# Large matmul operands placed at multiples of 256 bytes, and one preparation step moved, in a two-layer decoder trunk

## The chip, the cores and the metric

The kernel runs on one core of one Trainium2 chip. The metric is the device time of one execution in microseconds (us), the median of several runs. The profiled execution is one more run of the same program, with the hardware profiler on.

A core has a matrix engine (TensorE: PE for its products, PEld for its loads of the stationary operand), a vector engine (VectorE, DVE), an activation engine (ScalarE, ACT), GpSimd (POOL) and SyncE (SP), which here issues nearly all DMA transfers. A product of the matrix engine has a stationary operand of up to 128x128, loaded first, and a moving operand of 128 partitions and up to 512 columns, which streams through. Both are read from the on-chip memory (SBUF), which has 128 partitions; a tile has one address, the same in every partition. "At 64" below means an address that is 64 bytes past a multiple of 256.

## The reference

Two layers over 256 tokens of width 1024. Each layer runs four token mixers on the same input, gates and sums them, projects, and normalizes. Layer 0 then has a dense SwiGLU, layer 1 a mixture of eight experts, of which each token takes two. Both add a gated per-layer embedding.

```
for i in range(DEPTH):                       # 2
    h = x @ w_in[i]                          # 1024 x 6752
    ... s5, mla, hgrn2, retention            # four mixers, 256 wide each
    mixed = sum(gates * branches) @ w_o[i]
    x = layer_norm(ALPHA * x + mixed, ...)
    if i % 2 == 0:
        f = swiglu(x, ff_w_gate, ff_w_up, ff_w_down)       # 1024 -> 3584 -> 1024
    else:
        f = moe_swiglu(x, moe_router, moe_w_gate, moe_w_up, moe_w_down)  # 8 experts, top 2
    ple = sigmoid(x @ ple_w_gate[i]) * (p[i] @ ple_w_proj[i])
    x = layer_norm(ALPHA * x + f + ple, ...)
```

All inputs are float32.

## The kernel before

**Products.** Every large product is split in three. An operand is written as a high part `hi` in the type float32r and a rest `lo = x - hi`, also float32r; `mm3` (L246) issues hi·hi (L248), then one product with a `lo` (L249), then the other (L250), all into the same bank of PSUM. A float32r product reads 4 bytes per column and partition. In the four mixers' inputs, in the gates and in the dense SwiGLU's first part the weights are stationary and 256 columns of activations move; in the value and gate projections, the output projection, the dense second part and all of the experts 512 columns of weights move and the activations are stationary. Small products (attention scores, transposes, scans) are plain float32.

**Weights.** `Stream` (L132) carries the weights. A piece of 1 MB comes by DMA from SP into a slot `raw` (L157). `ahead` (L178) splits it: ACT writes `hi` (L191), DVE writes `lo` (L193). A slot of `raw` is reloaded as soon as its piece is split. In the experts' stage a piece is 128x2048, there are nine slots of `raw`, and four pairs `whi`, `wlo`; `whi` lies mostly in the pool `wp`, `wlo` in the pool `more`.

**Experts.** `experts` (L484) goes through 8 experts in four steps `j` of 8, 8, 8 and 4 pieces of gate and up products (`up`, bank `pff`), each followed by the down products of the step before (`down`, bank `pdn`, 4, 4, 4 and 2 pieces). That is 42 pieces of 12 products each per expert, 336 pieces and 4032 products in all, 2688 of them `pff` and 1344 `pdn`. The order of PE, DVE and ACT is here the order of the program (`manual_schedule`, L1797). After each piece `pump` (L226) lets the side generators go one step; a generator that yields n is left alone for n pieces. One side generator is `turn` (L1515), started after each `up`: it multiplies gate and up (L1517, DVE), transposes the result with PE (bank `ftp`, L1522) and splits it into `hth`, `htl`.

**The step that is moved.** `prepare` (L1651) readies the next expert's tokens. It is started before step 1 of an expert and must be done before the next expert's step 0 (`before`, L1807). In this order it builds a one-hot matrix on DVE (`oh`, L1656) with small copies on POOL (L1657), multiplies it with PE (`ohp`, L1662), copies the indices out (DVE, L1669; ACT, L1671), issues a gather of 128 rows from POOL (L1695), yields 6, and then twice transposes four blocks with PE (bank `gat`, L1687) and splits them on ACT and DVE (L565, L566) into `ghl`, the stationary operand of the next expert.

**Placement.** Pools are laid out one after the other, and a tile takes the next multiple of 32 bytes. On the left `cst` starts at 16512 and has 548 float32 columns; `mhalf` (L283), 32 bytes, follows at 18720; so the pool `wp` begins at 18752, which is at 64. `wp` and `act` hold multiples of 8192 bytes, so `raw`, `whi`, `xh`, `xl`, `ghl` and the rows are all at 64. The pool `sm` of small tiles has 2080 bytes, so that the pools of a stage behind it (the mixers' outputs `y`, `hth`, `htl`, the dense stage's additional `wparts`) are at 96. On the right, pools grow down from 229344, which is at 224: the S5 matrices, and in layer 1 the pool `more` with 11 slots of 8192 bytes (`wlo`, further `raw`) and two of 4096 (`ye`, among them the first expert's `gh`, `gl`) are at 224. The temporary tiles of the mixers are at 0, and only plain float32 products read them.

Of the kernel before, what the change touches and what calls it, by code (L numbers as in the profile page):

```python
# [10 lines left out]
F32 = mybir.dt.float32  # L11
F32R = mybir.dt.float32r
I32 = mybir.dt.int32
# [7 lines left out]
P = 128  # L21
T = 256
NT = 2
# [6 lines left out]
EPS = 1e-5  # L30
ALPHA = (2 * DEPTH) ** 0.25
MAGIC = 12582912.0


C_E = 0
# [62 lines left out]
def tile_trunk(ctx, tc, x, p, positions, w_in, s5_a_re, s5_a_im, s5_log_dt, s5_b_re, s5_b_im, s5_c_re, s5_c_im,  # L98
# [5 lines left out]
    V, G_, S, PE = nc.vector, nc.gpsimd, nc.scalar, nc.tensor  # L104
# [4 lines left out]
    const = ctx.enter_context(tc.tile_pool(name="const", bufs=1))  # L109
    wp = ctx.enter_context(tc.tile_pool(name="wp", bufs=1))  # L110
    act = ctx.enter_context(tc.tile_pool(name="act", bufs=1))
    sm = ctx.enter_context(tc.tile_pool(name="sm", bufs=4))
    drp = ctx.enter_context(tc.tile_pool(name="drp", bufs=1, space=bass.MemoryType.DRAM))
    ph = {}
    ps = ctx.enter_context(tc.tile_pool(name="ps", bufs=1, space=PSUM))

    def dump(name, ap):
        if dbg and name in dbg:
            nc.sync.dma_start(dbg[name], ap)

    def mm_bank(name):
        return ps.tile([P, 512], F32, tag="mm", bufs=4, name=name)

    def ax_bank(name):
        return ps.tile([P, 512], F32, tag="ax", bufs=4, name=name)
# [145 lines left out]
    mixc = mix_pool.__enter__()  # L271
# [8 lines left out]
    mcol = lambda c, n: cmix[:, c - C_MIX:c - C_MIX + n]  # L280
    m64 = mcol(C_M64, 2)
    m16 = mcol(C_M16, 2)
    mhalf = const.tile([P, 8], F32, name="mhalf")  # L283
    cols = mixc.tile([P, P], F32, name="cols")
    d_col = lambda i: cols[:, 64 + 8 * i:72 + 8 * i]
    qg_col = lambda i: (cols[:, 100 + i:101 + i], cols[0:64, 102 + i:103 + i])
# [12 lines left out]
    def reduce_angle(r, ang, k):  # L299

        V.tensor_scalar(k, ang, 1.0 / (2 * math.pi), MAGIC, op0=OP.mult, op1=OP.add)
        V.tensor_scalar(k, k, -MAGIC, None, op0=OP.add)
        V.scalar_tensor_tensor(r, k, -TWO_PI[0], ang, op0=OP.mult, op1=OP.add)
# [12 lines left out]

    stg = mixc.tile([P, P], F32, name="stg")
    sst = mixc.tile([P, 32], F32, name="sst")
    posi = mixc.tile([P, NT], I32, name="posi")

    def small_loads(q):

# [142 lines left out]
    def s5_setup(i, s5, pad, bank, turn):  # L465
# [82 lines left out]
            eng.tensor_tensor(o, o, w, op=op)  # L548
            yield 1
        yield 1  # L550
        toep = mixc.tile([P, 8, 4, 32], F32, tag="s5to", bufs=1, name="toep")
        yield from turn()
        for b2 in range(2):
            tb = bank("tb")
# [8 lines left out]
    def split_out(hi, lo, src, scale=None):  # L563
        if scale is None:
            S.activation(hi, src, AF.Copy)  # L565
            V.tensor_sub(lo, src, hi.bitcast(F32))  # L566
        else:
            S.activation(hi, src, AF.Copy, scale=scale)
            V.scalar_tensor_tensor(lo, src, scale, hi.bitcast(F32), op0=OP.mult, op1=OP.subtract)
# [621 lines left out]
    def mixers(i, xh, xl, s5, ready, end):  # L1191

        res, hl, rl = {}, {}, {}
        def prepare_s5():

            pad = act.tile([P, 2048], F32, tag="x", bufs=1, name="pad")
            yield from setup(ready, pad)
            yield from s5_setup(0, s5, pad, ax_bank, lambda: ())
# [68 lines left out]
        def branch(n, first=False, last=False):  # L1267
            drain_side(gens[n], "mixer %d of layer %d" % (n, i))
            y = res[n]
            dump("y%s%d" % ("abcd"[n], i), y[0].bitcast(F32))  # L1270
            if last:
                parts.extend(new_parts())
            for h in range(2):
                wh, wl = ws.take("br", n, i)
                for b in range(2):
                    o = mm_bank("pbr")
                    for f in range(2):
                        fs = slice((2 * b + f) * P, (2 * b + f + 1) * P)
                        for kk in range(2):
                            mm3(o[:, f * T:(f + 1) * T], wh[:, kk, fs], wl[:, kk, fs], y[0][:, kk, :], y[1][:, kk, :],  # L1280
                                kk == 0 and f == 0, kk == 1 and f == 1)
                    tv, av = flat(thg[n], 2 * h + b), flat(thg[ORDER[0]], 2 * h + b)
                    V.scalar_tensor_tensor(tv, tv, 1.0, o, op0=OP.add, op1=OP.mult)
                    if not first:
                        (V if last else G_).tensor_tensor(av, av, tv, op=OP.add)
                    if last:
                        split_out(flat(parts[0], 2 * h + b), flat(parts[1], 2 * h + b), av, 0.5)
                pump()
                finished()
            ph["branches"] += 1  # L1290
# [267 lines left out]
    def dense(i, xh, xl, pj, pr, gb, s5):  # L1558

        for c in range(4):  # L1560
            ple_quarter(i, c, xh, xl, pj, pr)
        res = []

        def add(tt, h, b):
            hs = slice(512 * h, 512 * h + 512)
            V.tensor_add(pr[:, tt, hs], pr[:, tt, hs], b)

        def end(u, todo):
            res.extend(ln_parts(pr, add, gb, todo, u["acc"], [fill0, lambda: drain_side(s5_)]))

        def turn():

            while not ph["spare"]:
                yield 1


        pad = ph["pool"].tile([P, 2, D], F32, tag="gain1", bufs=1, name="pad").rearrange("p a d -> p (a d)")
        s5_ = start_side(s5_setup(i + 1, s5, pad, mm_bank, turn))

        def fill0():  # L1580
            ph["spare"] = True
            for _ in range(4):
                step_side(s5_)


        ffn([dict(x=(xh, xl), take=lambda w, *k, **kw: ws.take(w, 0, *k, **kw))], NT, lambda n, j: None, end)
        return res
# [9 lines left out]
    def moe(i, xt, xh, xl, pj, pr, wr, more, gains, write):  # L1597
# [53 lines left out]
        def prepare(pcol, scol, wcol, e):  # L1651

            oh = ph["pool"].tile([P, NT, P], F32, tag="oh", bufs=1, name="oh")
            wt = sm.tile([P, NT, 2], F32, tag="wt", bufs=2, name="wt")
            for tt in range(NT):
                V.tensor_scalar(oh[:, tt, :], iota, pcol(tt), scol(tt), op0=OP.is_equal, op1=OP.mult)  # L1656
                G_.tensor_copy(wt[:, tt, 0:1], wcol(tt))  # L1657
                G_.tensor_copy(wt[:, tt, 1:2], cst[:, C_TOK + tt:C_TOK + tt + 1])
            yield 1
            tp = ax_bank("ohp")  # L1660
            for tt in range(NT):
                PE.matmul(tp[:, 256:258], oh[:, tt, :], wt[:, tt, :], start=tt == 0, stop=tt == 1)  # L1662
            if e.get("turned"):
                e["ohT"] = ohT = ph["pool"].tile([P, T], F32R, tag="ohT", bufs=1, name="ohT")
                for tt in range(NT):
                    PE.transpose(tp[:, tt * P:tt * P + P], oh[:, tt, :], ident)
            yield 1
            idx = sm.tile([P, 1], U32, tag="idx", bufs=2, name="idx")
            V.tensor_copy(idx, tp[:, 257:258])  # L1669
            e["ws"] = sm.tile([P, 1], F32, tag="ws", bufs=2, name="ws")  # L1670
            S.copy(e["ws"], tp[:, 256:257])  # L1671
            xg = rows_of(x_rows, idx, e.get("place", 0), "xg")
            if e.get("turned"):
                S.copy(ohT, tp[:, 0:256])
            yield 3 if e.get("first") else 6
            if e.get("first"):
                gh, gl = (ph["more"][0].tile([P, KD, P], F32R, tag="ye", bufs=2, name="g" + t) for t in "hl")
            else:

                both = act.tile([P, 2, KD, P], F32R, tag="xl" if e.get("odd") else "xh", bufs=1, name="ghl")  # L1680
                gh, gl = both[:, 0], both[:, 1]
            e["x"] = gh, gl
            for k4 in range(2):
                b = ax_bank("gat")
                for k in range(4):
                    ks = slice((4 * k4 + k) * P, (4 * k4 + k + 1) * P)
                    PE.transpose(b[:, k * P:(k + 1) * P], xg[:, ks], ident)  # L1687
                yield 1
                split_out(*(t[:, 4 * k4:4 * k4 + 4, :].rearrange("p k t -> p (k t)") for t in (gh, gl)), b)
                yield 1  # L1690

        def rows_of(src, idx, place, name):

            t = places[place]
            G_.indirect_dma_start(t, None, src[:, :], bass.IndirectOffsetOnAxis(ap=idx, axis=0))  # L1695
            return t
# [94 lines left out]

        for tt in range(NT):
            nc.gpsimd.dma_start(x_rows[tt * P:(tt + 1) * P, :], xt[:, tt, :])
        both_ = act.tile([P, NT, D], F32, tag="x", bufs=1, name="rows")
        places = [both_[:, n, :] for n in range(2)]
        state = {"p": start_side(first_rows())}
# [28 lines left out]
        with tc.If(many > P):  # L1825
# [4 lines left out]
            with tc.For_i(0, NE, 1) as ei:  # L1830
# [5 lines left out]
                more = Stream()  # L1836
# [51 lines left out]
    for i in range(DEPTH):  # L1888
# [33 lines left out]
        more = ph["more"] if last else (ph["pool"], "more", 2)  # L1922
# [3 lines left out]
        wr = router(i) if i % 2 else None  # L1926
        xt, xh, xl, pr = out_proj(i, mh, ml, xt, pj)
        dump("x1_%d" % i, xt)
        if i % 2 == 0:
            gb = gain_rows(ln2_g, ln2_b, i, (ph["pool"], "gain2", 1))  # L1930
# [3 lines left out]
        else:  # L1934
            moe(i, xt, xh, xl, pj, pr, wr, more, lambda: gain_rows(ln2_g, ln2_b, i, ws.free.pop(0)), write)
        dump("x2_%d" % i, pr)
        pool.__exit__(None, None, None)

# [31 lines left out]
```

## Time and profile before

| | us |
|---|---|
| median of 3 runs | 1856.11 |
| the runs | 1855.95 to 1862.53 |
| the profiled execution | 1855.93 |
| its span, first to last instruction | 1854.1 |

Columns and marks of the profile: "busy" is the time in which an engine has an instruction running. A product's duration includes its way through the array, and the next one starts long before it ends, so durations of products overlap and do not tell the pace; the distance of their starts does. In a timeline a row has the start, the length, the engine, the line and the operation, what is written from what, the shape, and how many were merged. "PE ... <- DVE ..." in a list of waits reads: PE waited for DVE.

### The profile page before, as it was taken

What the parts mean: (1) busy time and instruction counts of PE and PEld (TensorE: products, weight loads), DVE (VectorE), ACT (ScalarE), POOL (GpSimd) and SP (SyncE); (2) the same over time, 40 slices, a digit from 0 to 9 for tenths busy, and PEclk for the clock granted to TensorE, in tenths of its full rate; (3) what the DMA queues carried; (4) which work ended last, traced back from release to release, by engine and by line L of the source; (5) the groups of instructions that cost most, each with busy time, mean ns of one, the idle gap of its engine ahead of it and who ended that gap; (6) DMA issues with size and microseconds to landing.
All of it is one profiled execution on the core that took longest, in us unless ns stands there. A gap on an engine that the chain in (4) does not pass through costs nothing.

```text
span 1854.1 us, 25642 instructions
## 1 busy us (share of the span) xinstructions
PE 1798.2 (97%) x10285; PEld 1550.8 (84%) x10285; DVE 1443.1 (78%) x1344; ACT 1125.3 (61%) x1095; POOL 275.6 (15%) x286
## 2 busy tenths in 40 slices
PE   8999999999998999989999999999999999999996
PEld 7889989999987989978788788787887878878885
DVE  7966787645466965778888888888888888888896
ACT  5544455444445464546777777777776777777773
POOL 2746338100022210322000000000000000000001
PEclk9999999999999999999999999999999999999998
DMA  7443475555543346847999999999999999999991
GB/s 244 137 140 115 143 255 188 186 190 191 184 148 134 107 148 247 315 148 260 375 357 374 357 370 382 353 371 364 368 381 357 368 380 357 369 361 368 385 395 50
DMA packets 164115, 506.09 MB, mean 273 GB/s; under 512 B 15340, under 2 KB 30228, under 8 KB 149652
## 3 DMA queue, kind: packets, MB, share of 16 engines
q1 hardware_dynamic: 160900, 493.36, 72.7%
q0 software_dynamic: 2080, 7.35, 1.0%
q10 hardware_dynamic: 1008, 3.67, 0.5%
q8 instruction: 82, 1.34, 0.3%
q14 instruction: 45, 0.37, 0.1%
HBM read 497.52 MB, written 6.82 MB: 272 GB/s over the span
## 4 chain that ended last, share of the span: by engine, by line
PE 77%; DVE 5%; ACT 2%; issue 1%; POOL 0%; POOLq 0%; DVEq 0%; ACTq 0%
PE pff L248 14%; PE pff L250 14%; PE pff L249 14%; PE pdn L250 7%; PE pdn L248 7%; PE pdn L249 6%; PE pgt L250 2%; PE pgt L248 2%; PE pgt L249 1%; PE ftp L1522 1%; DVE wlo L193 1%; ACT whi L191 1%; DVE wparts L193 1%; DVE xt L603 1%; PE ppg L248 1%
## 5 line engine op out<-in xcount | busy, mean ns | idle before, releaser
L193 DVE TENSOR_TENSOR wlo<-raw,whi 128x2048 fp32r<-128x2048 f32 x336 | 768.5, 2292 | 129.3 <-ACT whi L191 120.4
L191 ACT ACTIVATE whi<-raw 128x2048 fp32r<-128x2048 f32 x336 | 643.4, 1918 | 244.5 <-PE pff L250 140.3
L193 DVE TENSOR_TENSOR wparts<-raw,wparts 128x1024 fp32r<-128x1024 f32 (+1 forms) x235 | 306.1, 1309 | 185.3 <-ACT wparts L191 184.3
L191 ACT ACTIVATE wparts<-raw 128x1024 fp32r<-128x1024 f32 (+1 forms) x244 | 254.4, 1049 | 252.3 <-PE pff L250 79.3
L248 PE MATMUL pff<-whi,ghl 128*128 128x512 f32 x784 | 312.8, 399 | 0.0
L250 PE MATMUL pff<-whi,ghl 128*128 128x512 f32 x784 | 309.1, 394 | 0.0
L249 PE MATMUL pff<-wlo,ghl 128*128 128x512 f32 x784 | 308.7, 394 | 0.0
L248 PE MATMUL pdn<-whi,hth 128*128 128x512 f32 x448 | 178.8, 399 | 0.0
L250 PEld LDWEIGHTS pff<-whi,ghl 128*128 128x128 f32 x784 | 147.2, 188 | 36.0
L250 PE MATMUL pdn<-whi,htl 128*128 128x512 f32 x448 | 177.0, 395 | 0.0
L249 PE MATMUL pdn<-wlo,hth 128*128 128x512 f32 x448 | 175.5, 392 | 0.0
L249 PEld LDWEIGHTS pff<-wlo,ghl 128*128 128x128 f32 x784 | 147.3, 188 | 33.7
L248 PEld LDWEIGHTS pff<-whi,ghl 128*128 128x128 f32 x784 | 147.2, 188 | 33.5
L250 PE MATMUL pgt<-xh,wparts 128*128 128x256 f32 x512 | 146.4, 287 | 1.7 <-DVE wparts L193 1.7
L249 PE MATMUL pgt<-xl,wparts 128*128 128x256 f32 x512 | 146.3, 286 | 0.0
L248 PE MATMUL pgt<-xh,wparts 128*128 128x256 f32 x512 | 146.2, 286 | 0.0
L249 PE MATMUL pff<-xl,wparts 128*128 128x256 f32 x448 | 126.4, 282 | 0.0
L248 PE MATMUL pff<-xh,wparts 128*128 128x256 f32 x448 | 126.3, 282 | 0.0
L250 PE MATMUL pff<-xh,wparts 128*128 128x256 f32 x448 | 126.3, 282 | 0.0
L250 PEld LDWEIGHTS pgt<-xh,wparts 128*128 128x128 f32 x512 | 98.5, 193 | 2.6 <-DVE wparts L193 1.9
L250 PEld LDWEIGHTS pdn<-whi,htl 128*128 128x128 f32 x448 | 84.2, 188 | 19.5
L249 PEld LDWEIGHTS pdn<-wlo,hth 128*128 128x128 f32 x448 | 84.3, 188 | 18.9
(570 smaller groups left out, 3135.4 us busy)
## 6 DMA issues: line engine op xcount, KB each, us to landing
raw<-in_moe_w_gate_dram SPq DMA_DIRECT2D x112, 1024.0 KB, 7.3
raw<-in_moe_w_up_dram SPq DMA_DIRECT2D x112, 1024.0 KB, 7.6
raw<-in_moe_w_down_dram SPq DMA_DIRECT2D x112, 1024.0 KB, 7.3
raw<-in_w_in_dram SPq DMA_DIRECT2D x49, 1024.0 KB, 5.0
raw<-in_ff_w_gate_dram SPq DMA_DIRECT2D x14, 1024.0 KB, 5.1
raw<-in_ff_w_up_dram SPq DMA_DIRECT2D x14, 1024.0 KB, 5.1
raw<-in_ff_w_down_dram SPq DMA_DIRECT2D x14, 1024.0 KB, 4.8
raw<-in_w_branch_dram SPq DMA_DIRECT2D x8, 1024.0 KB, 4.9
```

The source lines that it names most:

```text
L191: S.activation(hi, src, AF.Copy)
L193: eng.tensor_tensor(lo, src, hi.bitcast(F32), op=OP.subtract)
L248: PE.matmul(o, ah, bh, start=start, stop=False)
L249: PE.matmul(o, ah, bl, start=False, stop=False)
L250: PE.matmul(o, al, bh, start=False, stop=stop)
L603: V.scalar_tensor_tensor(dst[:, tt, hs], src[:, tt, hs], mv[:, 0:1], gb[0][h], op0=OP.subtract, op1=OP.mult)
L1522: PE.transpose(tp[:, c * P:(c + 1) * P], g[h][:, c, :], ident)
```

## The change

Two things are done. Five places get padding: `mhalf` grows from 8 to 56 columns (32 to 224 bytes), `sm` gets a tile of 224 bytes, `posi` grows by 8 columns, `toep` by 56, and the pool `more` gets a tile of 224 bytes, which comes behind its others. The new tiles are cleared with one DVE instruction each, so that they are used. And in `prepare`, for every expert but the first, a `yield 2` is put ahead of the one-hot matrix, and the `yield 6` after the gather becomes `yield 10`.

```diff
+PAD = 56
@@ tile_trunk
+    V.memset(sm.tile([P, PAD], F32, tag="pad", bufs=1, name="smpad"), 0.0)
@@
-    mhalf = const.tile([P, 8], F32, name="mhalf")
+    mhalf = const.tile([P, PAD], F32, name="mhalf")
@@
-    posi = mixc.tile([P, NT], I32, name="posi")
+    posi = mixc.tile([P, NT + 8], I32, name="posi")[:, 0:NT]
@@ s5_setup
-        toep = mixc.tile([P, 8, 4, 32], F32, tag="s5to", bufs=1, name="toep")
+        toep = mixc.tile([P, 1024 + PAD], F32, tag="s5to", bufs=1, name="toep")[:, 0:1024]
+        toep = toep.rearrange("p (g b c) -> p g b c", g=8, b=4)
@@ prepare
             wt = sm.tile([P, NT, 2], F32, tag="wt", bufs=2, name="wt")
+            if not e.get("first"):
+                yield 2
             for tt in range(NT):
@@
-            yield 3 if e.get("first") else 6
+            yield 3 if e.get("first") else 10
@@ moe
             nc.gpsimd.dma_start(x_rows[tt * P:(tt + 1) * P, :], xt[:, tt, :])
+        V.memset(ph["more"][0].tile([P, PAD], F32, tag="pad", bufs=1, name="morepad"), 0.0)
```

## Rows read from the trace of the kernel before

**Rows 1.** The page: busy time, share, instructions; the chain that ended last.
```profile
PE 1798.2 (97%) x10285; PEld 1550.8 (84%) x10285; DVE 1443.1 (78%) x1344; ACT 1125.3 (61%) x1095; POOL 275.6 (15%) x286
PE 77%; DVE 5%; ACT 2%; issue 1%; POOL 0%; POOLq 0%; DVEq 0%; ACTq 0%
```
**Rows 2.** Windows: length, busy PE PEld DVE ACT POOL, PE clock, DMA share, GB/s.
```profile
0.00:853.00 853.00, 822.34 (x5933) 761.57 (x5934) 586.73 (x817) 413.42 (x607) 250.34 (x247) 0.99 0.52 178
853.00:1835.00 982.00, 972.38 (x4348) 788.02 (x4346) 846.95 (x512) 710.40 (x486) 20.17 (x32) 1.00 0.95 360
```
**Rows 3.** Waits from 853 to 1835 us: total us, times, longest.
```profile
ACT whi L191 <- PE pff L250: 140.3, 163, 2.2
DVE wlo L193 <- ACT whi L191: 119.3, 208, 2.3
...
PE ftp L1522 <- DVE ghl L566: 8.9, 7, 1.4
```
**Rows 4.** Timeline of PE: one run of 96 `pff`, one of 47 `pdn`.
```profile
1709.15 0.39 PE L248 MATMUL pff<-whi,ghl 128*128 128x512 f32 x1
...
1731.27 0.39 PE L250 MATMUL pff<-whi,ghl 128*128 128x512 f32 x1
...
1823.98 0.40 PE L249 MATMUL pdn<-wlo,hth 128*128 128x512 f32 x1
...
1834.64 0.40 PE L250 MATMUL pdn<-whi,htl 128*128 128x512 f32 x1
```
**Rows 5.** Timeline of PE: 36 products of 512 columns, all operands at 64.
```profile
650.46 0.39 PE L248 MATMUL pqk<-wparts,xh 128*128 128x512 f32 x1
...
658.40 0.39 PE L250 MATMUL pqk<-wparts,xl 128*128 128x512 f32 x1
```
**Rows 6.** Timeline of PE: 192 products, then 96 with the moving operand at 96.
```profile
750.44 0.28 PE L248 MATMUL pgt<-xh,wparts 128*128 128x256 f32 x1
...
773.36 0.28 PE L250 MATMUL pgt<-xh,wparts 128*128 128x256 f32 x1
773.48 0.28 PE L248 MATMUL pbr<-ydh,wparts 128*128 128x256 f32 x1
...
784.67 0.28 PE L250 MATMUL pbr<-yah,wparts 128*128 128x256 f32 x1
```
**Rows 7.** Timeline of PE: 384 products of the dense stage's first part.
```profile
306.40 0.28 PE L248 MATMUL pff<-xh,wparts 128*128 128x256 f32 x1
...
352.06 0.28 PE L250 MATMUL pff<-xh,wparts 128*128 128x256 f32 x1
```
**Rows 8.** Plain float32 of 512 columns at 96: timeline, then the tile's duration.
```profile
1834.87 3.60 PE L1782 MATMUL cmb<-yef,ohT 128*128 128x512 f32 x8
...
L1782 PE MATMUL cmb<-yef,ohT x8: 590/592/595, 1834.9 to 1837.9; 128*128 128x512 f32 x8
```
**Rows 9.** Timeline of PE: products of 32 columns, paced by their weight loads.
```profile
169.84 0.39 PE L536 MATMUL kp<-pad,s5vr 128*128 128x32 f32 x2
...
170.51 0.39 PE L537 MATMUL kp<-pad,s5vi 128*128 128x32 f32 x2
```
**Rows 10.** Timeline of PE: the router, 8 stationary columns, 256 moving ones at 64.
```profile
826.67 0.28 PE L248 MATMUL lp<-xh,wrh 128*8 128x256 f32 x1
...
827.25 0.28 PE L250 MATMUL lp<-xh,wrl 128*8 128x256 f32 x1
```
**Rows 11.** Timelines of PE and of DVE where the prepared rows are split.
```profile
1032.04 0.60 PE L1522 MATMUL ftp<-cst,ffg 128*128 128x128 f32 x4
...
1027.79 2.29 DVE L193 TENSOR_TENSOR wlo<-raw,whi 128x2048 fp32r<-128x2048 f32 x1
1029.99 0.68 DVE L566 TENSOR_TENSOR ghl<-gat,ghl 128x512 fp32r<-128x512 f32 x1
1030.59 0.68 DVE L1517 TENSOR_TENSOR ffg<-ffg,pff 128x512 f32<-128x512 f32 x1
```
**Rows 12.** The tile `rows`, which the gathers write: us from issue to landing.
```profile
DMA to landing us min/median/max: 4.3/7.6/11.1
```

## The prediction

> **What bounds the kernel now.** I read the page first, to see which engine is never free: PE is busy 97% of the span and makes 77% of the chain that ended last [rows 1]. Then the windows, because a share of the whole span is a mean over stages: before the experts (0 to 853 us) PE is busy 822 of 853 us and DVE 587; with the experts (853 to 1835 us) PE is busy 972 of 982 us, DVE 847, and the DMAs 95% at 360 GB/s, at a granted clock of 1.00, which is 2.4 GHz [rows 2]. Three things are near their limit there, so the waits decide: ACT waits for PE to give a pair of weight parts back, DVE waits for ACT, and PE waits for nobody but 8.9 us in seven places; no wait of ACT for a weight's DMA is in the list [rows 3]. So PE sets the end, in both halves, and what counts is the pace of its products: the distance of their starts.
>
> That pace is read from the first and the last of a run. With the experts 96 `pff` take 22.12 us in 95 distances, 232.8 ns each, and 47 `pdn` 10.66 us in 46, 231.7 ns [rows 4]. 512 columns at 2.4 GHz are 213.3 ns, so each product carries some 19 ns beside its columns. Where all operands are at 64 the same shape takes 7.94/35 = 226.9 ns [rows 5]. With 256 columns (106.7 ns) it is 22.92/191 = 120.0 ns with everything at 64 and 11.19/95 = 117.8 ns with the moving operand at 96 [rows 6], and 45.66/383 = 119.2 ns in the dense stage, whose stationary parts are partly at 96 [rows 7]. So the surplus at 64 is 13.3 ns whether 256 or 512 columns move, it hangs on the placement, and no placement in the trace is without it: no moving float32r operand stands at a multiple of 256.
>
> **How large it is without a surplus.** Three rows bound it. Plain float32 products pass 512 columns at half the rate: eight take 3.60 us, the last 0.592, so (3.60-0.592)/7 = 430 ns against 426.7, 3 ns over, although both operands are at 96 [rows 8]. Changing the stationary operand therefore costs 3 ns, not 13; the rest of the surplus comes with reading 4 bytes per column at the full rate. Products of 32 columns show the pace of the weight loads alone: 0.67 us for six, 112 ns [rows 9]. And the router, which loads 8 columns instead of 128, still takes 0.58/5 = 116 ns for 256 columns moving from 64 [rows 10], 9 more than the columns: the moving operand's reading has a surplus with hardly a load beside it. 13.3 ns are 32 columns, 128 bytes: what one block more of 128 bytes would take, and a row of 1024 or 2048 bytes that begins at 64 touches one more such block than one at 0. That fits 120.0 = 288/2.4 and 226.7 = 544/2.4. I take this reading: at 0 the surplus goes, and 216 ns (213.3+3) remain for 512 columns, 112 for 256 (there the load's pace is the floor).
>
> **The change part by part.** *Padding.* `wp` moves from 18752 to 18944, which is 74 x 256; `sm` grows to 2304 bytes, so the stage pools follow from 96 to 0; on the right 224 bytes bring `more` from 224 to 0, and 256 bytes in all keep the mixers' temporary tiles at 0. So every float32r operand of a large product comes to 0.
> - Experts: 2688 x (232.8-216) + 1344 x (231.7-216) = 45.2 + 21.1 = 66 us. What is late next is DVE: its 847 us of work would stand in some 910, 93%, where a piece's 2.29 us [rows 11] must fit into 12 x 216 = 2.6 us beside the smaller instructions. I take 57 us of the 66. The DMAs would have to bring 390 GB/s instead of 360; no wait names them now [rows 2, 3], so I charge nothing, and up to 15 us if they fall behind.
> - Before the experts: 256 columns, 1824 gate and input products at 120.0, 1344 dense ones at 119.2, 768 branch and embedding products at about 117.8 [rows 6, 7]: 14.6 + 9.7 + 4.5 = 29 us. 512 columns: 288 at 226.9 and 576 between this and 232.8, say 230 [rows 4, 5]: 3.1 + 8.1 = 11 us. 96 products of 352 columns: 1 us. Together 41 us on PE. DVE and ACT chains of the mixers lie beside it, and PE is 31 us short of fully busy there [rows 2], so some of the gain turns into waits; I take three quarters, 31 us.
> - The two clearing instructions are 128x56; the nearest row is a split of 512 columns at 0.68 us [rows 11], so both cost between 0 and 1.4 us if uncovered. The first stands ahead of any data, the second beside products. Charged 0.
>
> *The step moved.* Per expert 1 to 7 it issues two one-hot instructions on DVE, four copies on POOL, the `ohp` products, an index copy on DVE, one copy on ACT, the gather from POOL, eight `gat` transposes, and two splits on ACT and DVE. Counted in pieces from its start, the one-hot goes from piece 1 to 3, the gather from 3 to 5, the transposes and splits from 9 to 12 to 15 to 18. There are 32 pieces until they are needed, so 14 remain. At 9 to 12 it meets `turn` of step 1, whose transposes need the product of L1517, and that stands on DVE behind the split of `ghl` [rows 11]: that is PE's 8.9 us, 7 times [rows 3]. At 15 to 18 no `turn` runs (one ends at 13, the next begins at 21). So 8 of the 8.9 us go. The gather lands 7.6 us, at most 11.1, after its issue [rows 12], far inside six pieces of 2.9 us, so the longer yield neither helps nor harms it. POOL does nothing else here (20 us busy of 982 [rows 2]), nothing is moved past SP's loads, and no wait is added on an engine.
>
> **Sum.** 57 + 31 + 8 = 96 us from the profiled 1855.93 us (span 1854.1), which stands with the median of 1856.11: 1760 us.
>
> **The rivals.**
> 1. *Only sameness counts.* The surplus would be a meeting of the moving row with the next weight load, set by their distance modulo 256. For: 226.9 with all at 64, 232.8 mixed. Then all at 0 is all at 64 again: the experts gain 2688 x 5.9 + 1344 x 4.8 = 22 us, 576 products 3 ns (2 us), while 2112 products of 256 columns lose up to 2.2 ns (3 us); with the step 22+2-3+8 = 29: 1827. Against: the router's 116 ns with 8 columns loaded [rows 10]. The Trainium skill, "SBUF — State Buffer", section "Who interferes with whom", gives PE two independent read ports, one for the moving operand and one for weight loads; by that rule this rival falls, but no run here shows the ports.
> 2. *Placement does nothing.* The differences between runs would come from their stage, not their address, and only the step's 8.9 us go: 1847. For: the two runs of 512 columns stand in different stages. Against: rows 6 change the pace from one product to the next, where only the moving operand's place changes. The Trainium skill, the same page, section "Specifications (TRN2)", names lines of 16 bytes as the unit that matters for bandwidth; every tile before the change starts at a multiple of 32, so by that rule nothing would change.
> 3. *Slower: everything meets.* With one phase for all operands each read could collide. For: 256 columns with all at 64 are slower (120.0) than with the moving operand at 96 (117.8) [rows 6]. Price: the same 2.2 ns again on 3936 products, 9 us, and the mixed pace of 512 columns worse by as much as 64-and-224 is worse than 64 alone, 5.9 ns on 4896, 29 us; less 8: 1886. It decides as soon as the experts' pace rises above 235 ns.
> 4. *DVE or the DMAs bind.* The pace falls to 216 in places, but the experts' stage gains only half, 33 us, and the mixers half, 20: 1795.
>
> **How the numbers follow.** Forecast 1760, its own range 1738 (all of 66, 41 and 9 us, and 2 for what is not seen) to 1785: 0.50. Rival 4: 0.12. Rival 1: 0.22. Rival 2: 0.09. Rival 3: 0.04. The rest, 0.03, is faster than 1738. The range 1738 to 1830 takes in the forecast and rivals 4 and 1, some 0.84. A measurement of this kernel can tell 0.5%, 9 us, from no change. Faster by more than that: 0.50+0.12+0.22+0.03, and of rival 2, which lies at the border, 0.03: 0.90. Same: 0.06. Slower: 0.04.
>
> **What would show it.** In the profile after, runs of `pff` and `pdn` should stand 216 to 219 ns apart, `pqk` 216, `pgt` 110 to 113; 226 and 120 would be rival 1, 232 and 119 rival 2, above 235 rival 3. The experts' stage should last some 915 us, with DVE above 90% and the DMAs near 385 GB/s; a wait of PE for `wlo`, or of ACT for `raw`, would be rival 4. `ftp` should no longer wait for `ghl`. The forecast is wrong if the surplus is a cost of full-rate reading that every placement pays.

## The result, and the profile after

The changed kernel takes 1832.08 us (median of 4 runs, 1829.64 to 1836.76) against 1856.04 us for the kernel before beside it: a ratio of 0.9861, 95% interval 0.9834 to 0.9888, 24 us less. A second measurement gave 1833.95 us and 0.9862 (0.9835 to 0.9889). The profiled execution took 1831.7 us, its span 1829.9. I had forecast 1760: the direction was right, three quarters of the gain did not come.

The page of the changed kernel (shares of the chain that ended last) answers to [rows 1]:

```profile
PE 79%; DVE 4%; ACT 1%; issue 1%; POOL 1%; POOLq 0%; DVEq 0%; ACTq 0%
```

Its windows, with the columns of [rows 2], are cut, to whole us, where the experts' first `pff` starts and their last `pdn` ends:

```profile
0.00:855.00 855.00, 824.77 (x5932) 765.30 (x5933) 590.55 (x819) 413.24 (x607) 246.90 (x247) 0.99 0.52 178
855.00:1811.00 956.00, 953.76 (x4349) 787.76 (x4348) 842.68 (x512) 708.93 (x486) 27.04 (x32) 1.00 0.96 369
```

PE is the bound as before. All of the gain lies in the experts: 982 us became 956, while the part before them went from 853 to 855. In the six profiles of trunk kernels below and above whose granted clock was 1.00 from 100 to 300 us, that first part took 851 to 855 us, so these 2 us are not read as a loss. (In the second measurement's profile it took 863.7 us, with a granted clock of 0.50, which is 1.2 GHz, from 200 to 210 us.)

The waits of the experts' stage (total us, times, longest), against [rows 3]:

```profile
ACT whi L194 <- PE pff L253: 117.4, 155, 1.7
...
PE ohp L1669 <- DVE oh L1663: 1.2, 2, 0.8
...
PE ftp L1527 <- DVE ffg L1522: 0.4, 2, 0.2
```

`ftp` no longer waits for `ghl` (8.9 us before). ACT still waits for PE to give weight parts back, and no wait for a weight's DMA is in the list.

The pace, first and last row of unbroken runs in the timeline of PE (start, length, line): 96 `pff` and 47 `pdn` of the experts [rows 4], 32 `pqk` [rows 5], 184 `pgt` and 96 `pbr` [rows 6].

```profile
1687.83 0.39 PE L251 MATMUL pff<-whi,ghl 128*128 128x512 f32 x1
...
1709.36 0.39 PE L253 MATMUL pff<-whi,ghl 128*128 128x512 f32 x1
...
1800.28 0.39 PE L252 MATMUL pdn<-wlo,hth 128*128 128x512 f32 x1
...
1810.76 0.39 PE L253 MATMUL pdn<-whi,htl 128*128 128x512 f32 x1
...
650.06 0.39 PE L252 MATMUL pqk<-wparts,xh 128*128 128x512 f32 x1
...
657.12 0.39 PE L253 MATMUL pqk<-wparts,xl 128*128 128x512 f32 x1
...
753.12 0.28 PE L252 MATMUL pgt<-xl,wparts 128*128 128x256 f32 x1
...
775.08 0.28 PE L253 MATMUL pgt<-xh,wparts 128*128 128x256 f32 x1
...
775.20 0.28 PE L251 MATMUL pbr<-ydh,wparts 128*128 128x256 f32 x1
...
786.60 0.28 PE L253 MATMUL pbr<-yah,wparts 128*128 128x256 f32 x1
```

`pff`: 21.53/95 = 226.6 ns (232.8 before). `pdn`: 10.48/46 = 227.8 (231.7). `pqk`: 7.06/31 = 227.7 (226.9). `pgt`: 21.96/183 = 120.0 (120.0). `pbr`, whose moving operand had stood at 96: 11.40/95 = 120.0 (117.8). With every operand at 0 the products have, within 1 ns, the pace that they had where every operand was at 64. No row shows the 216 and 112 ns of my forecast: these are the numbers that I had named for rival 1, "only sameness counts", whose time was 1827.

### The profile page after: what moved, and what is told of

The parts are those of the page before. It is cut to its first block, busy times and chain, and to the rows that moved or that the text cites. A ratio compares the mean times of both kernels' runs of the same rounds, so it can differ in the third digit from the quotient of the medians.

```text
span 1829.9 us, 25713 instructions
## 1 busy us (share of the span) xinstructions
PE 1782.1 (97%) x10285; PEld 1554.4 (85%) x10285; DVE 1442.6 (79%) x1346; ACT 1123.7 (61%) x1095; POOL 279.0 (15%) x286
## 4 chain that ended last, share of the span: by engine, by line
PE 79%; DVE 4%; ACT 1%; issue 1%; POOL 1%; POOLq 0%; DVEq 0%; ACTq 0%
PE pff L251 14%; PE pff L253 14%; PE pff L252 14%; PE pdn L251 7%; PE pdn L252 7%; PE pdn L253 7%; PE pgt L253 2%; PE pgt L251 2%; PE pgt L252 2%; PE ftp L1527 1%; DVE xt L608 1%; DVE wparts L196 1%; PE ppg L251 1%; PE ppg L253 1%; PE hgl L838 1%
## 5 line engine op out<-in xcount | busy, mean ns | idle before, releaser
L196 DVE TENSOR_TENSOR wparts<-raw,wparts 128x1024 fp32r<-128x1024 f32 (+1 forms) x235 | 312.5, 1337 | 184.5 <-ACT wparts L194 183.4
L251 PE MATMUL pff<-whi,ghl 128*128 128x512 f32 x784 | 310.0, 395 | 0.0
L253 PE MATMUL pff<-whi,ghl 128*128 128x512 f32 x784 | 305.7, 390 | 0.0
L253 PEld LDWEIGHTS pgt<-xh,wparts 128*128 128x128 f32 x512 | 98.4, 192 | 2.6 <-DVE wparts L196 1.9
L251 PEld LDWEIGHTS pgt<-xh,wparts 128*128 128x128 f32 x512 | 98.4, 192 | 0.8
```

Source lines behind the costliest of these rows:

```text
L196: eng.tensor_tensor(lo, src, hi.bitcast(F32), op=OP.subtract)
L251: PE.matmul(o, ah, bh, start=start, stop=False)
L253: PE.matmul(o, al, bh, start=False, stop=stop)
```

## The experiments

**Products alone, without a kernel around them.** The forecast's first half was a claim on one product, so it was measured by itself. The kernel's core, shortened:

```diff
+CASES: (name, m, s, n, c): moving at m, stationary at 16384 + s bytes of one tile
+    for r in range(33):
+        PE.matmul(b[0:c, 0:n], ab[:, s4:s4 + c], ab[:, m4:m4 + n], start=r == 0, stop=r == 32)
```

> This kernel holds nothing of the trunk: only runs of 33 products into one bank, read from copies of the inputs in float32r (and bfloat16). In a case's name n is the number of moving columns, m and s are the bytes past a multiple of 256 at which the moving and the stationary operand begin, c the stationary columns where they are not 128. Theory A (the distance between the two operands, modulo 256, sets the surplus): at m0s0, m32s32, m64s64, m128s128 all 512-column runs stand 227 ns apart and all 256-column runs 120 ns; at other distances the pace goes to both sides, 217 to 238 ns and 112 to 120 ns, and m64s0 is like m0s192. Theory B (my forecast: a block more when a row begins off a multiple of 256, or of 128): m0s0 and m128s128 216 and 112 ns, m32s32 and m64s64 227 and 120 ns, and s plays no part. Theory C (a fixed cost of reading 4 bytes per column at the full rate): 227 and 120 ns in every case, with 384 columns 173.3 ns. Under A with 8 stationary columns the surplus goes or halves (256 columns at 107 to 112 ns); under B and C it stays (116 to 120). bfloat16 should show 216 and 112 to 113 ns under all three.

Timeline of PE: each row is a case of 33 products, and the distance to the next row's start, over 33, is its pace (in the bfloat16 row the record of one product is missing). Each case ran once, at a mean granted clock of 0.997 here and 0.995 in the second set.

```profile
43.79 7.65 PE L64 MATMUL n512m0s0x<-ab 128*128 128x512 f32 x33
51.27 7.86 PE L64 MATMUL n512m0s32x<-ab 128*128 128x512 f32 x33
58.97 7.87 PE L64 MATMUL n512m0s64x<-ab 128*128 128x512 f32 x33
66.67 7.88 PE L64 MATMUL n512m0s96x<-ab 128*128 128x512 f32 x33
...
105.03 4.11 PE L64 MATMUL n256m0s0x<-ab 128*128 128x256 f32 x33
108.98 4.07 PE L64 MATMUL n256m0s32x<-ab 128*128 128x256 f32 x33
112.88 3.93 PE L64 MATMUL n256m0s64x<-ab 128*128 128x256 f32 x33
116.64 4.13 PE L64 MATMUL n256m0s96x<-ab 128*128 128x256 f32 x33
...
143.75 7.67 PE L64 MATMUL n512m64s64x<-ab 128*128 128x512 f32 x33
151.25 7.69 PE L64 MATMUL n512m128s128x<-ab 128*128 128x512 f32 x33
158.79 4.11 PE L64 MATMUL n256m32s32x<-ab 128*128 128x256 f32 x33
...
266.94 7.89 PE L64 MATMUL n512m224s64x<-ab 128*128 128x512 f32 x33
...
324.82 7.82 PE L64 MATMUL alt0y224x<-ab 128*128 128x512 f32 x33
332.49 7.82 PE L64 MATMUL alt0y64x<-ab 128*128 128x512 f32 x33
340.15 7.72 PE L64 MATMUL alt0y128x<-ab 128*128 128x512 f32 x33
347.71 7.86 PE L64 MATMUL alts0y32x<-ab 128*128 128x512 f32 x33
...
355.41 7.30 PE L64 MATMUL bf512x<-bb 128*128 128x512 bf16 x32
```

- 512 columns with both operands at 0: (51.27-43.79)/33 = 226.7 ns; both at 64: 227.3; both at 128: 228.5. Only the stationary one moved on by 32 or 64 bytes: 233.3.
- 256 columns, both at 0: 119.7; stationary 32 bytes on: 118.2; 64 bytes on: 113.9; 96 bytes on: 120.3 (118.8 when the same pair was run again in the second set, so differences of 1.5 ns between single cases prove little).
- bfloat16, 512 columns: 7.13/33 = 216 (the next case starts at 362.54).

So theory B, mine, falls: the bytes past a multiple of 256, or of 128, do nothing by themselves. A holds for the part between 226.7 and 233.3, but with 512 columns not for its lower side: no distance was better than 0. C fits the rest: no float32r case with 512 columns came below 226.7, 13.4 ns over the 213.3 of its columns, while bfloat16, with as many moving and stationary columns, has 2.7 (its loads are shorter too, 98 ns instead of 188 by the trace; the second set shows that this is not the cause).

`alt0y224x` tells why the mixed pace was as high as it was: every third product alone moves from another place (by 160 bytes, the distance of 224 from 64), and the mean of all is 7.67/33 = 232.4, not (2x226.7+233.3)/3 = 228.9. So one strange operand in three can slow its neighbours too: at 64 bytes it does so as well (232.1), at 128 it does not (229.1), and a stationary operand 32 bytes off in every third product gave 233.3, as if all were off. In the kernel before, one piece in four had `whi` in the pool `more` too, at 224 like `wlo`; alone such products take (274.67-266.94)/33 = 234.2 (the next case starts at 274.67), and in the kernel every fourth group of 12 stood 234 to 235 ns apart. Then (3x232.4+234.2)/4 = 232.8, which is the pace of `pff` before the change, with nothing left over.

**A second set of the same kind**, for the distance of 64 and for the load (shortened).

```diff
+    k256: moving ab[:, m4 + 256 * (r % 8):], stationary ab[:, 4096 + s4 + 128 * (r % 4):]
+    f512, f256: the same tiles read as plain float32
+    n512m0s0c8: 8 stationary columns
```

> Again only runs of 33 products and nothing of the trunk; in names beginning with n both operands stay where they are, in names beginning with k both go on by whole blocks from product to product as in the kernel, in names beginning with f the type is plain float32. The first such kernel left two things: with 256 columns the pace was 119.7 ns at equal places but 113.9 with the stationary operand 64 bytes behind, and no float32r case came under 113.9 (256 columns) or 226.7 (512), while bfloat16 had 216 and 109. Theory A+C (a fixed cost of reading 4 bytes per column at the full rate, and on top a meeting of the two readings that hangs on their distance): 113 to 115 ns at every distance of 64 whatever the base (m64s128, m128s192, m192s0, and 64 plus multiples of 256), k256m0s64 114 ns against 119.7 for k256m0s0; 512 columns stay at 226.7 or above for distances of 16 bytes and more; plain float32 430 and 217 ns at every place. Rival (the 113.9 is a matter of one pair of addresses): the other distances of 64 lie at 117 to 120 ns, and so does k256m0s64. With 8 stationary columns and 512 moving ones: 220 to 223 ns if the load takes part, 226.7 if it does not.

```profile
167.66 7.64 PE L54 MATMUL n512m0s240x<-ab 128*128 128x512 f32 x33
...
182.84 7.64 PE L54 MATMUL n512m0s0c8x<-ab 128*8 128x512 f32 x33
190.32 7.81 PE L54 MATMUL n512m0s0c32x<-ab 128*32 128x512 f32 x33
197.97 7.74 PE L54 MATMUL n512m0s0c64x<-ab 128*64 128x512 f32 x33
205.55 4.12 PE L54 MATMUL k256m0s0x<-ab 128*128 128x256 f32 x33
209.50 4.05 PE L54 MATMUL k256m0s64x<-ab 128*128 128x256 f32 x33
...
243.96 28.48 PE L54 MATMUL f512m0s0x<-ab 128*128 128x512 f32 x66
272.28 28.49 PE L54 MATMUL f512m0s32x<-ab 128*128 128x512 f32 x66
```

With 8 stationary columns instead of 128 the pace is the same 7.48/33 = 226.7 ns, although such a load lasts 88 ns instead of 188: the 13.4 are not the load. Its width is not without effect, though: with 32 and 64 stationary columns the pace is 231.8 and 229.7, and with 256 moving columns at equal places 8 and 64 stationary ones gave 115.8 and 113.6 in the first set, against 119.7. Plain float32 (two records for a product) takes 28.32/66 = 429 ns per record, 2.4 over its columns at half the rate. So the 13 ns belong to float32r at the full rate, as theory C has it; whether to its 4 bytes per column or to the type, and what they are made of, isn't shown. Nor is equality the only good place: with the stationary operand 240 bytes on, 512 columns also took 226.7 (the next case starts at 175.14). On the distance of 64 the rival was half right: held in place, the six pairs with 64 between them gave 113.3 to 113.9 or 117.6 to 117.9 ns, never anything between, and with operands that go on 117.9 (the next case starts at 213.39). So the distance alone does not settle the pace.

**The two parts of the change, each alone** (shortened).

```diff
 step alone: the kernel before, and
+            if not e.get("first"):
+                yield 2
-            yield 3 if e.get("first") else 6
+            yield 3 if e.get("first") else 10
 padding alone: the five paddings and no line of these
```

> The moved step without the padding; all tiles stand as before the change. If the wait of ftp for ghl is worth its 8.9 us: 1847 to 1849 us, experts' products still at 232 ns, that wait under 1 us. If the wait only goes elsewhere: 1856 us.

> The padding without the moved step. Theory A (only sameness counts, 22 us in the experts, about zero before them): 1836 to 1840 us, the experts' products at 227 ns, and the wait of ftp for ghl still there with some 9 us. Theory B': the padding is worth all of the 24 us and the moved step nothing: 1832 us.

The step alone: 1849.54 us, ratio 0.9958 (0.9943 to 0.9974). The padding alone: 1838.19 us, 0.9907 (0.9881 to 0.9933). The product of the two, 0.9865, is the whole change's 0.9861 well within the intervals: no sign that they touch each other. The experts' window of the step alone, then that of the padding alone with the wait that stays in it:

```profile
851.00:1824.00 973.00, 971.31 (x4346) 787.60 (x4345) 843.57 (x512) 708.91 (x486) 24.70 (x32) 1.00 0.95 363
```

```profile
852.00:1814.00 962.00, 951.92 (x4339) 786.43 (x4338) 845.99 (x512) 710.12 (x486) 22.23 (x32) 1.00 0.96 367
...
PE ftp L1527 <- DVE ghl L571: 9.4, 7, 1.5
```

From the first start to the last end the stage lasts 981.8 us before, 973.4 with the step and 963.2 with the padding (whose window above is 1.2 us short of that): the step takes 8.5 and the padding 18.7. In the padding alone PE stands idle for 10 us of the window, as before; in the step alone for 1.7.

**All operands at 64 instead of at 0.**

```diff
-    mhalf = const.tile([P, PAD], F32, name="mhalf")
+    mhalf = const.tile([P, 8], F32, name="mhalf")
-        toep = mixc.tile([P, 1024 + PAD], F32, tag="s5to", bufs=1, name="toep")[:, 0:1024]
+        toep = mixc.tile([P, 1024 + 40], F32, tag="s5to", bufs=1, name="toep")[:, 0:1024]
-        V.memset(ph["more"][0].tile([P, PAD], F32, tag="pad", bufs=1, name="morepad"), 0.0)
+        V.memset(ph["more"][0].tile([P, 40], F32, tag="pad", bufs=1, name="morepad"), 0.0)
```

> The change with less padding, so that every operand of a large product is at 64 past a multiple of 256 instead of at 0. Theory A (sameness): as the changed kernel, 1829 to 1836 us, experts' products at 227 ns, gate products at 120 ns. If multiples of 256 count as such: slower than the changed kernel by 2 to 20 us, experts' products at 228 to 232 ns.

1830.28 us, ratio 0.9864 (0.9838 to 0.9890), the changed kernel's own. Its 96 `pff`:

```profile
1685.86 0.39 PE L251 MATMUL pff<-whi,ghl 128*128 128x512 f32 x1
...
1707.40 0.39 PE L253 MATMUL pff<-whi,ghl 128*128 128x512 f32 x1
```

21.54/95 = 226.7 ns. Nothing is special about multiples of 256: operands that agree at 64 do as well.

**One padding only.** Rival 1 says that one tile of 160 bytes, which brings the pool `more` to where `ghl` is, gives `pff` its gain and `pdn` none.

```diff
 the kernel before with the moved step, and
+        V.memset(ph["more"][0].tile([P, 40], F32, tag="pad", bufs=1, name="morepad"), 0.0)
```

> The kernel before with the moved step and one padding only: a tile of 160 bytes that brings the pool of wlo (and of half of whi) from 224 to 64, where the rest already stands. Then pff has all three operands at 64; the stationary operands of pdn stay at 96. If the step that the change owes its gain to is the pff sameness (2688 x (232.1-227.3) = 13 us): pff at 227 ns, pdn at 231 ns, 1836 to 1838 us. If multiples of 256 or the other places were needed: pff above 229 ns and 1843 us or more.

1836.62 us, ratio 0.9891 (0.9867 to 0.9916). Its 96 `pff` and 47 `pdn`:

```profile
1690.71 0.39 PE L248 MATMUL pff<-whi,ghl 128*128 128x512 f32 x1
...
1712.25 0.40 PE L250 MATMUL pff<-whi,ghl 128*128 128x512 f32 x1
...
1803.89 0.40 PE L249 MATMUL pdn<-wlo,hth 128*128 128x512 f32 x1
...
1814.62 0.40 PE L250 MATMUL pdn<-whi,htl 128*128 128x512 f32 x1
```

`pff` 21.54/95 = 226.7 ns, `pdn` (stationary at 96, both moving parts at 64) 10.73/46 = 233.3, 2 more than I had expected: the two sorts of product in one trace, 6.6 ns apart, where in the changed kernel, with all at 0, they are 1.2 apart.

**My pace, brought about otherwise.** The second half of my sum said how much of a faster PE arrives at the end. That can be tried without a better placement, by moving fewer columns.

```diff
+        n = o.shape[1]
+        n = {512: 472, 256: 232}.get(n, n)
         PE.matmul(o, ah, bh, start=start, stop=False)
-        PE.matmul(o, ah, bl, start=False, stop=False)
-        PE.matmul(o, al, bh, start=False, stop=stop)
+        PE.matmul(o[:, 0:n], ah, bl[:, 0:n], start=False, stop=False)
+        PE.matmul(o[:, 0:n], al, bh[:, 0:n], start=False, stop=stop)
```

> The changed kernel with the pace that I had forecast, brought about in another way: the two products with a rest (hi by lo, lo by hi) move 472 of 512 and 232 of 256 columns, the first of the three stays whole; the part that is left out is that of the rests in the last columns. By 227 ns and a passing 2.4 columns per ns a set of three takes 227+2x210.3, 215.9 ns each, and with 256 columns 119.9+2x112, 114.6 each. If PE alone sets the end, as the second half of my sum had it (57 of 66 us and 31 of 41): the experts' stage goes from 955 to 911 to 917 us, the part before it from 855 to 826 to 833 us, 1760 to 1775 us. If DVE or the DMAs bind at this pace (my rival 4): the experts' stage 925 to 940 us with PE waiting for wlo or ACT for raw.

1780.57 us, ratio 0.9579 (0.9555 to 0.9603), above the 1760 to 1775 of the first reading. The pace came to (1671.25-1650.34)/95 = 220.1 ns in a run of 96 `pff`, not to 215.9. That unequal lengths cost these 4 ns isn't shown: 472 columns were not run alone, and with 256 and 232 columns the dense `pff` came below the 114.6 expected, at (355.75-312.34)/383 = 113.3. Those rows, the experts' window and the longest wait of PE in it:

```profile
1650.34 0.39 PE L253 MATMUL pff<-whi,ghl 128*128 128x512 f32 x1
...
1671.25 0.37 PE L255 MATMUL pff<-whi,ghl 128*128 128x472 f32 x1
...
840.00:1771.00 931.00, 922.92 (x4343) 786.31 (x4342) 840.09 (x512) 706.13 (x486) 45.05 (x32) 1.00 0.97 379
...
PE ftp L1529 <- DVE ffg L1524: 5.5, 6, 1.7
```

PE saves 4032 x (227.0-220.1) = 28 us of products (227.0 is the mean of the 226.6 and 227.8 of the changed kernel, two to one), and the stage goes from 956 to 931, 25 us. So most of a gain in pace does arrive. What is late next is DVE, as I had put it, and one can see where: PE waits 5.5 us for `ffg`. The DMAs bring 379 GB/s, and neither ACT's wait for `raw` nor PE's for `wlo` is in the list. So the 931 us lie where I had put rival 4 (925 to 940) without its waits: what is missing is the pace that didn't come, 4032 x 4.2 = 17 us. Rival 4 doesn't decide at this pace; at 216 ns it was not tried. For the part before the experts this profile is no measure: 840 us, but with a granted clock of 0.50 (1.2 GHz) from 195 to 205 us. By the medians beside each other, 1833.95-1780.57-25 = 28 us came outside the experts, where PE saved some 3936 x 6.6 + 864 x 7 = 32 us: an estimate.

**A try for more: apart where 256 columns move.** In `mm3` with 256 columns the weights are stationary, and equal places are among their slowest (119.7 above). Shortened:

```diff
 everything at 64 (mhalf 8, toep 1024, sm's pad 24, more's pad 40 columns), and
-        return [act.tile([P, KD, T], F32R, tag=t, bufs=1, name=t) for t in ("xh", "xl")]
+        ts = [act.tile([P, KD * T + 48], F32R, tag=t, bufs=1, name=t)[:, c:c + KD * T] for t, c in (("xh", 48), ("xl", 0))]
+        return [t.rearrange("p (k t) -> p k t", k=KD) for t in ts]
 ghl in the same tiles, cut so that it stays at 64
```

> A try for a faster version: all operands of the experts at 64 as in the run with everything at 64, but xh and xl, which move 256 columns at a time past weights before the experts, at 0, 64 bytes from the weights. From the runs of products alone (117.9 instead of 119.7 ns with 256 columns, 229.4 instead of 227.3 where the same tiles are stationary and 512 columns of weights move): 3168 x 1.8 = 5.7 us less, 864 x 2.1 = 1.8 us more on PE: 4 us at best, 1826 to 1832 us. If the distance plays no part in the kernel: gates at 120 ns and the time of the changed kernel.

> The changed kernel itself, beside the three others on the same chip: 1829 to 1836 us.

1822.05 us, ratio to the kernel before 0.9813 (0.9790 to 0.9835), beside 1833.95 for the changed kernel on the same chip: 12 us better than the change by the medians, 8 by the lowest runs (1820.40 and 1828.14). The part before the experts, then its runs of `pgt` and of the dense `pff`:

```profile
0.00:845.00 845.00, 813.35 (x5936) 753.34 (x5937) 586.58 (x819) 413.66 (x608) 251.20 (x247) 0.99 0.54 180
...
744.46 0.28 PE L252 MATMUL pgt<-xl,wparts 128*128 128x256 f32 x1
...
765.20 0.28 PE L253 MATMUL pgt<-xh,wparts 128*128 128x256 f32 x1
...
304.56 0.28 PE L251 MATMUL pff<-xh,wparts 128*128 128x256 f32 x1
...
349.67 0.28 PE L253 MATMUL pff<-xh,wparts 128*128 128x256 f32 x1
```

`pgt` 20.74/183 = 113.3 ns, `pff` 45.11/383 = 117.8, against 120.0: the same two values as in the products alone. 1344 x 2.2 = 3 us for the dense part, 1824 times 2.2 to 6.7 = 4 to 12 for the rest, less 864 x 2 for 512 columns: 5 to 13 us. In the profiles that part went from 855 to 845 us, and the experts stayed (956 and 955). I had expected 4 at best, because I had counted with 117.9 alone.

## Why the prediction was wrong, point by point

**What bounds the kernel: right.** PE makes 79% of the chain, and its pace is what the time follows; in the runs with padding or with fewer columns the gain of the experts' stage was that of its products but for 2 to 4 us, and in the run of the step alone it was the wait that went.

**The step that failed** is the size of what placement can take away. "What bounds the kernel now" ends with a surplus of 13.3 ns that "hangs on the placement", and "How large it is without a surplus" takes the reading that at 0 "the surplus goes". [rows 6] had shown that placement moves 2.2 ns of it with 256 columns, and [rows 4, 5] 5.9 with 512, on top of the 13.3; I let it carry all 13.3, because 128 bytes and 32 columns fitted. Shown since: equal places give 226.7 to 228.5 ns whatever the place, equal places at 64 give the whole kernel its changed time, and 13 ns remain in every 512-column case. [rows 10] was read rightly in that the load is not the cause with 512 columns (8 columns loaded, 226.7 ns), and wrongly as a matter of where the row begins; with 256 columns the load does take part (115.8 ns with 8 columns loaded, 119.7 with 128). [rows 8] too: "the rest of the surplus comes with reading 4 bytes per column at the full rate" fits all that was measured since, and is no reason to think that it ever goes. The prediction's own last sentence names what came: a cost of full-rate reading that every placement pays.

**The terms.**
- Experts, 57 us from the padding: 19 measured. The differences that were real are 6.2 ns for `pff` and 3.9 for `pdn`: 2688 x 6.2 + 1344 x 3.9 = 22 us, and that is rival 1's term; why 3 of them did not arrive is open.
- Before the experts, 31 us: none that can be seen (853 and 855 us). With 256 columns the pace is 120.0 before and after where all stood at 64; what had stood apart got slower (`pbr` from 117.8 to 120.0).
- The step, 8 us: 9 us of the stage in the run of the step alone, 1856.21-1849.54 = 6.7 us of the median (the interval is 5 to 11). `ftp`'s wait went, and `ohp` waits 1.2 us for `oh` instead, which I had not listed. This term was right.
- How much of PE's gain arrives, 57 of 66: 25 of 28 in the run with fewer columns, at a smaller gain. Right in kind.

**The rivals.** Rival 1 had the mechanism and nearly the time: 1827 against 1832. Of the 30 us that it had in the experts, 26 came. Against it I had held the router and two read ports. 32 bytes of distance between the moving and the stationary operand cost 6.6 ns per product with 512 columns, so the two do meet somewhere; whether at a port isn't shown. The Trainium skill, "SBUF — State Buffer", section "Who interferes with whom", gives the moving operand and the weight loads read ports of their own. Where that would make their places independent, the measurement decides against it. Rival 2 falls as well: a shift of the stationary operand alone by 32 bytes moved the pace from 226.7 to 233.3. The Trainium skill, "SBUF — State Buffer", section "Specifications (TRN2)", has lines of 16 bytes as the unit that matters for bandwidth. That shift is a multiple of 16 bytes, so this unit doesn't suffice to judge a placement here. Rival 3's collision of equal places is true for 256 columns (119.7, among the slowest) and the opposite of true for 512.

**The range** ended at 1830, 3 us above rival 1, as if that rival's own terms were exact; its 22 us were 3 too large.

## What to carry to other kernels

A difference between two paces in a trace proves as much as it measures: 2 ns by place don't show that 13 ns are place. Where a forecast rests on what one instruction would do at a place that the trace doesn't have, price the change by the best pace that the trace does have, and count anything beyond as a chance. For float32r products of 512 columns put moving and stationary operands at the same distance from a multiple of 256 bytes, all of them, since one that differs can slow its neighbours; for 256 columns put them 64 bytes apart (113.3 to 117.9 ns here, against 119.7).

## What was not expected of the hardware

- A float32r product costs 13 ns beside its 512 columns, at equal places, with 8 or 128 stationary columns (with 32 or 64, 18 and 16); bfloat16 and plain float32 cost 2.4 to 2.7 there.
- Moving and stationary operand meet by their distance: 226.7 ns at 0 and at 240, 233.3 at 32 or 64 bytes with 512 columns; 119.7, 118.2 and 113.3 to 117.9 ns at 0, 32 and 64 with 256.
- At a distance of 64 with 256 columns there are two rhythms, 113.3 and 117.8 ns, for what looks like the same work (`pgt` and the dense `pff` of the last run). What chooses between them is open; 1344 x 4.5 = 6 us hang on it in this kernel.
